# Four FF2 sections a layer and one more block pair in a two-layer decoder trunk

## The chip, the cores and the metric

The kernel runs on one core of a Trainium2 chip. The metric is device time in microseconds of one execution. TensorE (PE) multiplies, VectorE (DVE) and ScalarE (ACT) split, evacuate and activate, GpSimd (POOL) issues accumulating DMAs and takes a few small powers, and SyncE (SP) issues the plain DMAs.

## The reference

Sequence 512, model width 1024, FF width 2816, float32 throughout. Layer 0 mixes with dilated attention, layer 1 with causal pooling; each is followed by a SwiGLU block, which is where the change lies:

```python
def swiglu_ffn(h, w_gate_up, w_down):
    gu = h @ w_gate_up
    gate, up = gu[..., :D_FF], gu[..., D_FF:]
    return (jax.nn.silu(gate) * up) @ w_down

def reference(x, ...):
    for i in range(DEPTH):
        ...  # x = x + mixer(rmsnorm(x, g))
        x = x + swiglu_ffn(rmsnorm(x, ffn_norm[i]), w_ffn_gate_up[i], w_ffn_down[i])
    return rmsnorm(x, final_norm)
```

## The kernel before

**Arithmetic.** A float32 product is made of three products of rounded parts: every weight and every operand is split into a high part and a low rest (`split`: ACT writes the high part, DVE the rest), and `hi*hi`, `hi*lo`, `lo*hi` are added in PSUM. A *plain* product takes matmuls of 128x128 weights against 512 columns (`Product.add`). A *block* product (`chained`, with `mult`) works on 2x2 blocks and needs seven products of half size, with 256 columns each, instead of eight; in return ACT and DVE form sums of blocks of the weights and of the results.

**The FFN.** The width 2816 is 22 chunks of 128. `gate_up(j)` makes chunk j of the hidden activation: for j < `NPLAIN` as a plain pair (`plain_pair`: two plain products, 48 matmuls of 512 columns), else as a block pair (`strassen_pair`, 84 matmuls of 256 columns). FF2, the product with `w_down`, runs in sections given by `PARTS[layer]`, each `(first, end, block)`: gate/up runs up to the section's end (one chunk further before a block section), and then `down` adds the section's part of FF2 to the residual X. A plain section makes eight products (one per 128 output rows); a block section makes four `chained` calls, for two output chunks each. Block gate/up needs the normed input as blocks, which `prepare(k)` makes in four steps on DVE and ACT; a block FF2 section needs the hidden chunks as blocks (`operands`, `operands_right`, `operands_left`), which are put off (`late`) and run inside the next `chained`.

**Weights.** All weight tiles come through four rings: `raw` (4 buffers of 128x1024, where DMAs land), `rawhalf` (2), `w` (5 buffers for the split weights) and `half` (2). A plain unit is one load and one split. A block pair (`Pair`) is three SP loads `b`, `a`, `c`, a fourth, accumulating DMA issued by POOL that adds to `b` after it has landed, and four splits: `blocks` (of a), `sums` (of the accumulated b), `more` (a plus b, two DVE adds ahead of the split) and `last` (of c):

```python
nc.sync.dma_start(self.b, self.src[:, :2 * n])
nc.sync.dma_start(self.a, self.src[:, n:3 * n])
nc.sync.dma_start(self.c, self.src[:, :n])
nc.gpsimd.dma_start(self.b.rearrange("p (a c) -> p a c", a=2),
                    self.src[:, None, 3 * n:].to_broadcast([P, 2, n]), accum_op=OP.add)
```

`chained` uses them in the order b, s, m, b, s, m, l (first half of `blocks`, first half of `sums`, first half of `more`, then the second halves, then `last`).

**Order.** The source lists all units in the order of their use (`ffn_plan`). `pump`, called after each product, issues the loads whose buffers are free in the program's order and up to two splits; a scheduler then orders the instructions of each engine at build time, and each engine runs its own list in that order. A load waits on the chip until the last reader of its buffer (a DVE instruction) is done, and a split until the last matmul that reads its `w` buffer is.

**The end.** FF2's last section in layer 1 ends with two output chunks in halves of 256 columns (`ends`, `end`, `add`), so that the final norm and the output of the left half run beside the right half's products; `emit` scales and stores the left half, `turn_last` and the code after it transpose and store the right half.

Of the kernel before, what the change touches and what calls it, by code (L numbers as in the profile page):

```python
# [15 lines left out]
P = 128  # L16
S = 512
D = 1024
# [45 lines left out]
def trunk(ctx: ExitStack, tc: tile.TileContext, xT, norms, w_first, w_qk, w_qkp, w_v0, w_v0p, w_v12, w_out, w_pair, w_down, w_dblock, w_pin, w_pgrp,  # L64
# [171 lines left out]
    def ffn_plan(layer):  # L236
        j = 0
        for i, (first, end, block) in enumerate(PARTS[layer]):
            while j < min(end + block, FC):
                if j < NPLAIN:  # L240
                    plain_gu(layer, j)
                else:
                    pairs(w_pair[layer, j], shift=0, back=True)
                j += 1
            if block:
                for m in range(K2):
                    pairs(w_dblock[sum(p[2] for l in range(layer) for p in PARTS[l]) + sum(p[2] for p in PARTS[layer][:i]), m],
                          shift=0, back=True)
# [733 lines left out]
    with tc.tile_pool(name="fpool", bufs=2) as fpool:  # L982
# [24 lines left out]
        def ffn(layer, nxt, lead, row):  # L1007
# [6 lines left out]
            def plain_pair(j, up):  # L1014
                pg = gu()
                gt = ftile("gt")
                nc.vector.tensor_mul(gt, pg, row)
                pu = gu()
                if j == NPLAIN - 1:
                    for k in range(KC):  # L1020
                        give((op, k))
                nc.vector.tensor_mul(up, pu, row)
                nc.scalar.activation(gt, gt, AF.Silu)
                nc.vector.tensor_mul(up, up, gt)
# [89 lines left out]
            def gate_up(j, ahead):  # L1114
                first, block = next((p[0], p[2]) for p in PARTS[layer] if p[0] <= j < p[1])
                u = tmp.tile([P, S], F32, tag="sq", name="u", bufs=3) if block or ahead else ftile("up")
                i, odd = (j - first) // 2, j % 2
                if j < NPLAIN:
                    plain_pair(j, u)
                elif block and odd and j == FC - 1:  # L1120
                    strassen_pair(u, later(operands, i, U["even"]), later(operands_right, i, u))
                else:
                    strassen_pair(u)
                if j == FC - 1:
                    for key in [key for key in held if key[0] == "t"]:
                        give(key)
                if ahead and not block:
                    U["later"] = j, u
                elif not block:
                    keep(j, u)  # L1130
                elif not odd:
                    U["even"] = u
                elif j == FC - 1:
                    operands_left(i, u)
                else:
                    late.extend([later(operands, i, U["even"]), later(operands_right, i, u), later(operands_left, i, u)])
                if j < K2:
                    prepare(j)

# [9 lines left out]
            for first, end, block in PARTS[layer]:  # L1149
                while j < min(end + block, FC):  # L1150
                    gate_up(j, j == end)
                    j += 1
# [4 lines left out]
                if block:  # L1157
# [108 lines left out]

        ends = [[weights() for n in units_of(HALF)] for i in range(2)]
        halves = [slice(i * S // 2, (i + 1) * S // 2) for i in range(2)]

        def end(i, half, js, f=None):  # L1270
            f = f or Product(HALF, hidden, keep=ends[i])
            return f.add(js, cols=halves[half])

        def add(i, half, f):
            m, cols = KC - 2 + i, halves[half]
            nc.vector.tensor_add(X[m][:, cols], X[m][:, cols], f.p[:, cols])
# [34 lines left out]

        def total(half, sq):
            t = ftile("total", H2)
            nc.vector.tensor_add(t, acc[4][:, halves[half]], sq)
            return t
# [12 lines left out]
        turn_last(range(5))  # L1328
        sq = add(1, 1, f)
        scale_last(KC - 1, on_dve=True)  # L1330
# [93 lines left out]
```

## Time and profile before

| | |
|---|---|
| median of 3 runs | 1206.85 us (1206.4 to 1207.08) |
| profiled execution, its own time | 1206.44 us |
| its span | 1204.6 us |
| PE busy | 1193.7 us, 9720 matmuls |
| DVE busy | 966.3 us |
| ACT busy | 658.0 us |
| POOL busy | 138.7 us |
| HBM | 151 GB/s over the span |

Busy times are of the span of one profiled execution; the execution itself takes 1.8 us longer than the span. A row of a timeline gives the start in us from the start of the span, the duration, the engine, the line of the kernel, the operation, what it writes and reads, and in brackets how long the engine idled before it and what released it. SPq and POOLq are issues of DMAs. In a table of windows each engine has its busy time in the window with the number of instructions, then follow the TensorE clock that was granted (1.00 is full), the DMA share and the rate.

Where the parts of the program lie in the span: attention and its output projection up to 481 us, layer 0's FFN up to 806, the pooling mixer up to 874, layer 1's FFN and the final norm to the end.

### The profile page before, as it was taken

The page shows a single profiled execution, that of the slowest core. Times are in us where ns is not written, and L with a number is a line of the kernel's source. Part 1 is how long each engine was busy: PE and PEld are TensorE (multiplying, and loading weights), DVE is VectorE, ACT ScalarE, POOL GpSimd, SP SyncE. Part 2 cuts the span into 40 slices and gives each one's busy share as a digit, 9 for nine tenths or more (in the row PEclk, how much of TensorE's full clock was granted, in tenths as well). Part 3 has the DMA queues.
Part 4 walks back from the last instruction along what each step waited for, and adds up shares of the span by engine and source line. Part 5 has one row for each costly group of instructions (what it writes and reads, how often), then busy time and mean ns, then how long its engine had stood idle before and what let it go on. Part 6 is the DMA issues. An engine that isn't in the chain of part 4 may idle for free.

```text
span 1204.6 us, 24247 instructions
## 1 busy us (share of the span) xinstructions
PE 1193.7 (99%) x9720; PEld 1117.6 (93%) x9720; DVE 966.3 (80%) x1650; ACT 658.0 (55%) x1162; POOL 138.7 (12%) x131
## 2 busy tenths in 40 slices
PE   9999999999999999999999999999999999999997
PEld 7889999999999988888999999988788999999987
DVE  7888888878889854965898889989997898788633
ACT  6545554555556543542677567663443676566531
POOL 1111111111111100101111111000300111111000
PEclk9999999999999999999999999999999999999999
DMA  8346667666756532336677777644016677777322
GB/s 292 112 103 171 144 158 169 162 166 150 179 150 158 190 123 91 96 106 142 177 199 192 186 196 192 182 149 140 28 53 166 162 196 187 192 192 190 110 77 71
DMA packets 71152, 183.65 MB, mean 152 GB/s; under 512 B 7152, under 2 KB 8320, under 8 KB 71040
## 3 DMA queue, kind: packets, MB, share of 16 engines
q1 hardware_dynamic: 49824, 140.41, 35.7%
q0 software_dynamic: 21072, 41.43, 20.9%
q8 instruction: 76, 1.25, 0.4%
q14 instruction: 36, 0.29, 0.1%
q10 hardware_dynamic: 144, 0.26, 0.1%
HBM read 179.98 MB, written 2.10 MB: 151 GB/s over the span
## 4 chain that ended last, share of the span: by engine, by line
PE 91%; DVE 5%; issue 2%; ACT 1%; POOL 0%; DVEq 0%; POOLq 0%; DMA 0%; ACTq 0%
PE ps L424 17%; PE ps L425 17%; PE ps L426 17%; PE ps L294 9%; PE ps L295 9%; PE ps L297 9%; PE ps L595 2%; PE ps L597 2%; PE ps L596 2%; DVE w L93 1%; PE ps L807 1%; PE ps L679 1%; DVE s L1223 1%; PE ps L699 1%; PE ps L801 1%
## 5 line engine op out<-in xcount | busy, mean ns | idle before, releaser
L92 ACT ACTIVATE w<-raw 128x1024 fp32r<-128x1024 f32 (+3 forms) x303 | 309.8, 1028 | 258.3 <-PE ps L297 84.3
L93 DVE TENSOR_TENSOR w<-raw,w 128x1024 fp32r<-128x1024 f32 (+3 forms) x303 | 356.1, 1180 | 76.3 <-ACT w L92 72.3
L424 PE MATMUL ps<-far,w 128*128 128x256 f32 x860 | 236.7, 275 | 0.0
L425 PE MATMUL ps<-far,w 128*128 128x256 f32 x860 | 236.7, 275 | 0.0
L426 PE MATMUL ps<-far,w 128*128 128x256 f32 x860 | 236.6, 275 | 0.0
L425 PEld LDWEIGHTS ps<-far,w 128*128 128x128 f32 x860 | 161.5, 188 | 0.1
L424 PEld LDWEIGHTS ps<-far,w 128*128 128x128 f32 x860 | 161.5, 188 | 0.1
L426 PEld LDWEIGHTS ps<-far,w 128*128 128x128 f32 x860 | 161.4, 188 | 0.0
L424 PE MATMUL ps<-near,w 128*128 128x256 f32 x556 | 158.1, 284 | 1.5 <-ACT first L506 1.5
L425 PE MATMUL ps<-near,w 128*128 128x256 f32 x556 | 154.3, 278 | 0.0
L426 PE MATMUL ps<-near,w 128*128 128x256 f32 x556 | 154.3, 277 | 0.0
L295 PE MATMUL ps<-near,w 128*128 128x512 f32 (+1 forms) x364 | 137.7, 378 | 0.6 <-DVE near L357 0.6
L294 PE MATMUL ps<-near,w 128*128 128x512 f32 (+1 forms) x364 | 138.1, 380 | 0.0
L297 PE MATMUL ps<-near,w 128*128 128x512 f32 (+1 forms) x364 | 137.3, 378 | 0.0
L424 PEld LDWEIGHTS ps<-near,w 128*128 128x128 f32 x556 | 104.8, 188 | 2.5 <-ACT first L506 2.1
L425 PEld LDWEIGHTS ps<-near,w 128*128 128x128 f32 x556 | 104.6, 188 | 0.0
L426 PEld LDWEIGHTS ps<-near,w 128*128 128x128 f32 x556 | 104.5, 188 | 0.0
L160 POOL DMA_DIRECT2D raw<-w_pair x34 | 41.2, 1210 | 366.5 <-DMA raw<-w_pair 200.1
L295 PEld LDWEIGHTS ps<-near,w 128*128 128x128 f32 x364 | 68.5, 188 | 14.0 <-DVE near L357 1.7
L297 PEld LDWEIGHTS ps<-near,w 128*128 128x128 f32 x364 | 68.5, 188 | 12.8
L294 PEld LDWEIGHTS ps<-near,w 128*128 128x128 f32 x364 | 68.5, 188 | 12.5
L92 ACT ACTIVATE half<-rawhalf 128x512 fp32r<-128x512 f32 x75 | 47.2, 631 | 14.4 <-PE ps L426 12.3
(323 smaller groups left out, 2671.1 us busy)
## 6 DMA issues: line engine op xcount, KB each, us to landing
raw<-w_pair SPq DMA_DIRECT2D x78, 512.0 KB, 4.5
raw<-w_qkp SPq DMA_DIRECT2D x36, 512.0 KB, 4.2
raw<-w_pair POOLq DMA_DIRECT2D x34, 512.0 KB, 7.4
raw<-w_dblock SPq DMA_DIRECT2D x24, 512.0 KB, 4.1
raw<-w_v SPq DMA_DIRECT2D x18, 512.0 KB, 4.4
raw<-w_qkp POOLq DMA_DIRECT2D x18, 512.0 KB, 7.6
rawhalf<-w_pair SPq DMA_DIRECT2D x34, 256.0 KB, 5.1
raw<-w_dblock POOLq DMA_DIRECT2D x12, 512.0 KB, 7.5
```

Source lines behind the costliest of these rows:

```text
L92: nc.scalar.activation(hi, v, AF.Copy)
L93: nc.vector.tensor_tensor(lo, v, hi.bitcast(F32), op=OP.subtract)
L160: nc.gpsimd.dma_start(self.b.rearrange("p (a c) -> p a c", a=2), self.src[:, None, 3 * n:].to_broadcast([P, 2, n]), accum_op=OP.add)
L294: nc.tensor.matmul(self.p[:, cols], w[0][:, s], mh[:, cols], start=self.done == 0, stop=False)
L295: nc.tensor.matmul(self.p[:, cols], w[0][:, s], ml[:, cols], start=False, stop=False)
L297: nc.tensor.matmul(self.p[:, cols], w[1][:, s], mh[:, cols], start=False, stop=self.done == self.n)
L424: nc.tensor.matmul(dst, w.t[0][:, c], th, start=k == 0 and not on, stop=False, skip_group_check=on)
L425: nc.tensor.matmul(dst, w.t[0][:, c], tl, start=False, stop=False, skip_group_check=on)
L426: nc.tensor.matmul(dst, w.t[1][:, c], th, start=False, stop=k == n - 1, skip_group_check=on)
L595: nc.tensor.matmul(o, mh, wh, start=k == 0, stop=False)
L596: nc.tensor.matmul(o, mh, wl, start=False, stop=False)
L597: nc.tensor.matmul(o, ml, wh, start=False, stop=k == K2 - 1)
```

## The change

Layer 0's FF2 sections become 2 plain, 8 block, 6 block and 6 plain chunks (before: 6 plain, 8 block, 8 block); layer 1's become 2 plain, 8 block, 8 block and 4 plain (before: 4 plain, 8 block, 10 plain). The plain gate/up pairs of a layer go from five to four, so chunk 4 is now a block pair. All plain pairs now run before the first FF2 section (`max(end + block, NPLAIN)`), and `prepare(j)` stands inside plain pair j, between its gate and its up product, not behind the pair. At the end five output chunks, not two, are made in halves, and the squares of all five are summed half by half. On the host the block weights of a 6-chunk section are padded to the width of the others; the loads take only the used part.

```diff
-NPLAIN = 5
+NPLAIN = 4
...
-PARTS = {0: ((0, 6, False), (6, 14, True), (14, 22, True)), 1: ((0, 4, False), (4, 12, True), (12, 22, False))}
+PARTS = {0: ((0, 2, False), (2, 10, True), (10, 16, True), (16, 22, False)),
+         1: ((0, 2, False), (2, 10, True), (10, 18, True), (18, 22, False))}
+ENDS = 5
...
-            while j < min(end + block, FC):
+            while j < min(max(end + block, NPLAIN), FC):
...
                 for m in range(K2):
-                    pairs(w_dblock[...section..., m],
-                          shift=0, back=True)
+                    pairs(w_dblock[...section..., m, :,
+                                   :2 * (end - first) * P], shift=0, back=True)
...
             def plain_pair(j, up):
                 pg = gu()
                 gt = ftile("gt")
                 nc.vector.tensor_mul(gt, pg, row)
+                prepare(j)
                 pu = gu()
...
-                if j < K2:
-                    prepare(j)
...
-                while j < min(end + block, FC):
-                    gate_up(j, j == end)
+                while j < min(max(end + block, NPLAIN), FC):
+                    gate_up(j, block and j == end)
                     j += 1
...
-                for m in range(KC - 2 if nxt == 4 and last else KC):
+                for m in range(KC - ENDS if nxt == 4 and last else KC):
...
-        t = total(0, add(0, 0, end(0, 0, range(HALF))))
-        sq = add(1, 0, end(1, 0, range(HALF)))
-        f = end(0, 1, range(5))
+        t, late = (acc[4][:, cols] for cols in halves)
+        for i in range(ENDS):
+            sq = add(i, 0, end(i, 0, range(HALF)))
+            if i < ENDS - 1:
+                t = total(t, sq)
+        f = end(0, 1, range(HALF))
         r = rstd([t, sq])
-        end(0, 1, range(5, HALF), f)
-        t = total(1, add(0, 1, f))
-        f = end(1, 1, range(1))
+        t = total(late, add(0, 1, f))
+        t = total(t, add(1, 1, end(1, 1, range(HALF))))
+        f = end(2, 1, range(HALF // 2))
         emit(0, r)
-        for k in range(KC - 1):
+        for k in range(KC - ENDS + 2):
             scale_last(k)
-        f = end(1, 1, range(1, HALF), f)
+        t = total(t, add(2, 1, end(2, 1, range(HALF // 2, HALF), f)))
+        f = end(3, 1, range(HALF))
+        scale_last(KC - 3)
+        t = total(t, add(3, 1, f))
+        f = end(4, 1, range(HALF))
+        scale_last(KC - 2)
         turn_last(range(5))
-        sq = add(1, 1, f)
+        sq = add(4, 1, f)
         scale_last(KC - 1, on_dve=True)
```

More of the change, by code (lines that the diff above doesn't have):

```diff
@@ L246, in ffn_plan @@
                 for m in range(K2):
-                    pairs(w_dblock[sum(p[2] for l in range(layer) for p in PARTS[l]) + sum(p[2] for p in PARTS[layer][:i]), m],
-                          shift=0, back=True)
+                    pairs(w_dblock[sum(p[2] for l in range(layer) for p in PARTS[l]) + sum(p[2] for p in PARTS[layer][:i]), m, :,
+                                   :2 * (end - first) * P], shift=0, back=True)
             else:
@@ L1264, in trunk @@
         hidden, HALF = ffn(1, 4, lead, row)
-        ends = [[weights() for n in units_of(HALF)] for i in range(2)]
+        ends = {}
         halves = [slice(i * S // 2, (i + 1) * S // 2) for i in range(2)]
         def end(i, half, js, f=None):
+            if i not in ends:
+                ends[i] = [weights() for n in units_of(HALF)]
             f = f or Product(HALF, hidden, keep=ends[i])
@@ L1274, in add @@
         def add(i, half, f):
-            m, cols = KC - 2 + i, halves[half]
+            m, cols = KC - ENDS + i, halves[half]
             nc.vector.tensor_add(X[m][:, cols], X[m][:, cols], f.p[:, cols])
```

14 lines of the change are left out of this document (7 added, 7 removed).

## The prediction

> **What bounds the kernel now.** I read the page's totals and chain first, then stretches of the span with the granted clock, then single rows where a plain FF2 section hands over to block work.
>
> ```profile
> span 1204.6 us, 24247 instructions
> PE 1193.7 (99%) x9720; PEld 1117.6 (93%) x9720; DVE 966.3 (80%) x1650; ACT 658.0 (55%) x1162; POOL 138.7 (12%) x131
> PEclk9999999999999999999999999999999999999999
> ...
> PE 91%; DVE 5%; issue 2%; ACT 1%; POOL 0%; DVEq 0%; POOLq 0%; DMA 0%; ACTq 0%
> ```
>
> TensorE (PE) is busy for 99% of the span, at full clock in nearly every slice, and is 91% of the chain that ended last. So a change pays by what it takes off PE, and costs what it makes PE wait. What a matmul costs is read from stretches without waits.
>
> ```profile
> 486.28 0.39 PE L295 MATMUL ps<-near,w 128*128 128x512 f32 x1
> ...
> 499.21 0.39 PE L295 MATMUL ps<-near,w 128*128 128x512 f32 x1
> ...
> 600.00:785.00 185.00, 184.29 (x1617) 184.09 (x1616) 167.39 (x292) 126.25 (x226) 21.77 (x18) 1.00 0.73 191
> 944.00:1120.00 176.00, 176.00 (x1547) 176.00 (x1546) 150.94 (x250) 118.10 (x199) 21.73 (x18) 1.00 0.71 187
> ```
>
> Between the first two rows lie 57 starts of 512-wide matmuls: 12.93 / 57 = 0.2268 us each. The last row is a stretch of 256-wide matmuls alone (block work in layer 1): 176 / 1547 = 0.1138 us each. The third column is PE, the fifth DVE: 151 of 176 us, and 167 of 185 us in the stretch of layer 0. DVE is near PE there, but below it.
>
> **The change: work of PE.** Chunk 4 turns from a plain gate/up pair into a block pair, one a layer, and trades 48 wide matmuls for 84 narrow ones. Layer 0's FF2 goes from 16 block chunks to 14 (+48 wide, -84 narrow), layer 1's from 8 to 16 (-192 wide, +336 narrow). The halves at the end are 120 narrow matmuls before (2 chunks x 2 halves x 10 x 3) and after (5 x 2 x 4 x 3). In sum +420 narrow and -240 wide, which the order of the built program also gives: 420 x 0.1138 - 240 x 0.2268 = 47.8 - 54.4 = **-6.6 us**. All of it is on the path, since PE sets it.
>
> **A wait that goes.** Layer 0 ends before in a block section in which each step also carries the next norm's work on DVE; after, it ends in six plain chunks (4.1 us of PE per output chunk, 18 x 0.2268).
>
> ```profile
> L424 PE MATMUL ps<-near,w 128*128 128x256 f32 x556 | 158.1, 284 | 1.5 <-ACT first L506 1.5
> ```
>
> These 1.5 us of idle PE (three waits between 775 and 797 us) lie in that section: **-1.5 us**, from 0 if the next late thing takes their place.
>
> **A wait that comes: the first block pair after the short FF2 section.** After the change both layers run four plain pairs, then FF2 over two chunks, then the first block pair (chunk 4). Let T be the end of the last plain up product. FF2 over two chunks is 8 x 2 x 3 = 48 wide matmuls, 10.9 us; the pair's first product takes 12 x 0.1138 = 1.4 more. So PE wants the second product's weights, the "sums" of a pair, at T+12.3. Before, layer 0's first block pair came straight behind five plain pairs, its loads long issued, and layer 1's behind 21.8 us of FF2 (96 wide) and a plain pair.
>
> These sums need a chain that can't start early. The pair loads into the ring of four "raw" buffers behind the eight FF2 units; its first load (b) takes the buffer of unit five, whose split waits for the "w" buffer of the last gate/up weight, free at T. The nearest place in the trace is layer 1 after its first FF2 section, where the same steps run:
>
> ```profile
> 905.91 0.68 DVE L1022 TENSOR_TENSOR up<-ps,row 128x512 f32<-128x512 f32 x1
> 906.54 0.69 DVE L93 TENSOR_TENSOR w<-raw,w 128x512 fp32r<-128x512 f32 x1
> ...
> 912.39 0.69 DVE L93 TENSOR_TENSOR w<-raw,w 128x512 fp32r<-128x512 f32 x1
> 913.10 0.33 SPq L157 DMA_DIRECT2D raw<-w_pair  x1
> 915.33 0.33 SPq L158 DMA_DIRECT2D raw<-w_pair  x1
> 916.66 1.06 ACT L92 ACTIVATE w<-raw 128x1024 fp32r<-128x1024 f32 x1 [2.09 <-PE ps L297]
> 917.75 1.23 DVE L93 TENSOR_TENSOR w<-raw,w 128x1024 fp32r<-128x1024 f32 x1 [0.45 <-ACT w L92]
> 918.16 1.23 POOL L160 DMA_DIRECT2D raw<-w_pair  x1 [43.34 <-DMA raw<-w_pair]
> 919.01 0.33 SPq L157 DMA_DIRECT2D raw<-w_pair  x1
> 927.05 0.69 DVE L176 TENSOR_TENSOR raw<-raw 128x512 f32<-128x512 f32 x1 [2.67 <-DMA raw<-w_pair]
> ```
>
> The split ends at 913.08 and SP issues b at 913.10: the load does wait for the ring. POOL's accumulating DMA follows at 918.16 (5.1 us: it waits for b to land), and DVE has its result at 927.05 (8.9 us). Of all accumulating DMAs, and of the two in this window:
>
> ```profile
> DMA to landing us min/median/max: 6.4/7.5/10.3
> ...
> DMA to landing us min/median/max: 6.6/7.7/8.8
> ```
>
> Now the chain after the change. Unit five's split follows the up multiply (905.91 to 906.54, 0.6 us) and has 256 columns instead of 512 (0.35 us), so b goes out at T+1.0. Accumulate issued: T+6.1. Landed: T+14.9, with the 8.8 of the nearest place, where as here three more loads follow at once. ACT's half of the split 1.06: T+16.0. DVE's half 1.23: T+17.2. PE, which wanted it at T+12.3, stands 4.7 us in all.
>
> Then "more": two adds, with one X add between them, a split on ACT and one on DVE.
>
> ```profile
> L176 DVE TENSOR_TENSOR raw<-raw x1: 692/692/692, 927.0 to 927.0; 128x512 f32<-128x512 f32 x1
> L177 DVE TENSOR_TENSOR raw<-raw x1: 684/684/684, 928.3 to 928.3; 128x512 f32<-128x512 f32 x1
> ```
>
> 0.69 + 0.69 + 0.68 + 1.06 + 1.23 = 4.35 us, in which PE has only 24 narrow matmuls (2.7 us) and a few that stand interleaved (0.8): about 0.9 us more. Behind these splits in ACT's queue stand two more weight splits (2.1 us) and then the copy that frees the PSUM tile for the pair's fifth product, some 0.5 us late.
>
> One more wait follows from ACT's order in the built program. The split of the third pair's sums stands ahead of the second pair's first copy. The third pair's b takes the first pair's b buffer, free after its first add (T+17.9): issue T+18.0, accumulate T+23.1, landed T+30.6 (median 7.5; few other loads now), split T+31.7, copy T+32.0. PE, now 6 us late, wants it at T+29.5: 2.5 us. The fourth pair's chain is in time. Per layer 4.7 + 0.9 + 0.5 + 2.5 = 8.6 us, from 5.6 (landing 6.6 throughout) to 10.2 (8.8 throughout). Two layers: **+17 us**, 11 to 20.
>
> A rule of the Trainium skill speaks here: "DMA: Bandwidth & Descriptors", section "Anatomy of one DMA — SWDGE (gpsimd) path", puts a POOL-issued DMA at about 2.0 us plus its bytes over 436 GB/s, so 512 KB would be an estimated 3.2 us, which would take the stall away. The trace does not agree: no accumulating DMA landed in less than 6.4 us.
>
> **Clock.** Waits of several us are new to PE here.
>
> ```profile
> 1198.00:1200.00 2.00, 0.00 (x1) 0.00 (x0) 1.41 (x2) 1.27 (x2) 1.05 (x2) 0.94 0.21 71
> 1200.00:1204.60 4.60, 0.00 (x0) 0.00 (x0) 0.00 (x1) 0.00 (x0) 0.00 (x0) 0.50 0.61 228
> ```
>
> After PE's last matmul at 1198 the granted clock is 0.94 over two us and then 0.50: it can halve within two us of idling. How long it stays low once PE resumes no row shows. From nothing (the idle is short, and PE waits again anyway) to the 2.7 us of work between two waits run at half speed (2.7 us a layer): I take **+1 us** for both layers, 0 to 5.4. The skill's "TensorE: Matmul & The Clock Gate", section "Part 1: The HAM clock gate", has an idle window of about 3.4 us, free-running; by it the 3.7 us wait would halve the clock in many runs.
>
> **The rest.** Preparation moves inside the pairs: the same instructions, in the built order now all ahead of the last up multiply, where before three splits of 512 columns (0.6 us each, by the row at 906.54) came behind it. Against these 1.8 us DVE saves 0.25 us on each of four narrower FF2 splits and has a pair's 10.9 us of PE work as cover. Cost 0; if the cover failed, up to 1.8 us a layer. Layer 1's further block sections load DVE as in the 944 to 1120 stretch: 0. At the very end DVE's eight output scalings stand ahead of the last three adds, before it was one:
>
> ```profile
> 1193.02 2.83 DVE L1287 SCALAR_TENSOR_TENSOR x<-x,nrm,ps 128x256 f32<-128x256 f32 x7
> 1195.76 0.41 DVE L1276 TENSOR_TENSOR x<-x,ps 128x256 f32<-128x256 f32 x1
> ```
>
> The last add began where the scalings ended; two more adds and totals may lengthen the tail: **+0.5 us**, 0 to 1.5.
>
> **Sum.** The profiled execution took 1206.44 us (span 1204.6), 0.4 under the median of 1206.85. 1206.4 - 6.6 - 1.5 + 17 + 1 + 0.5 = 1216.8; beside the median **1217 us**.
>
> **Rivals.**
> 1. *Faster: the accumulate lands in time.* The first split must be ready at T+12.3, so the landing may take 12.3 - 1.06 - 6.1 = 5.1 us at most; then only -6.6 - 1.5 + 0.5 remain: 1199. Against it, the smallest of 75 is 6.4; for it, the DMA queues are emptier than on average. Chance 0.10.
> 2. *Half the wait.* PE's interleaved matmuls, or loads released earlier than I read, cut the stall to 4 us a layer: 1206.4 - 8.1 + 8.5 = 1207. Chance 0.08.
> 3. *More waits.* ACT's order makes a third pair wait, or DVE (167 of 185 us in layer 0's block stretch) becomes the bound over layer 1's new block section; 8.8 us throughout (+20), the clock's full 5.4 and the tail's 1.5 give 1225; a DVE that is 3% too slow over 150 us of block work adds 4.5 more. Chance 0.15.
>
> **How the numbers follow.** The forecast has 0.67, and its own range runs from 1210 (11 us of stall) to 1221. The range that leaves out under 2 in 10 reaches from rival 2 to rival 3: 1207 to 1226; below lie rival 1 and a little. A difference under 0.2% (2.4 us) can't be told from none. Faster: 0.12 (rival 1 and the low part of rival 2); same 0.04; slower 0.84.
>
> **What would show it.** In the changed profile: two PE waits of over 2 us a layer, at the second product of chunk 4's pair and the third of chunk 5's, put down to ACT's weight split and copy, with POOL's accumulate landing 6.5 to 9 us after issue; DVE and ACT idle there too; 420 more narrow and 240 fewer wide matmuls; no PE wait at layer 0's end. If PE runs through chunk 4 without a wait, the prediction is wrong.

## The result: 1225.6 us against 1206.6, and where the profile shows the loss

The changed kernel takes 1225.60 us (median of 4 runs, 1224.94 to 1228.61) against 1206.62 us before (4 runs, 1206.27 to 1207.08). The ratio is 1.0161, 95% interval 1.0148 to 1.0173. The forecast was 1217, with 1207 to 1226 as its range: the side was right and the stall was where it was placed, but 9 us were missing. The profiled execution took 1225.7 us. Its page has these totals and this chain:

```profile
span 1223.9 us, 24860 instructions
PE 1198.1 (98%) x9900; PEld 1128.4 (92%) x9900; DVE 1002.9 (82%) x1747; ACT 680.2 (56%) x1227; POOL 146.7 (12%) x137
PEclk9999999999999999989999999999999999999999
...
PE 82%; DMA 6%; DVE 6%; issue 3%; ACT 1%; POOL 1%; POOLq 0%; DVEq 0%; ACTq 0%; SPq 0%
```

PE has 180 matmuls more (420 narrow more, 240 wide fewer), and one slice of the span shows a clock below 0.9. DMA, 0% of the chain that ended last before, is 6% of it now: PE waits for loads. The stretches of the span show where. First after, then before (columns: stretch, PE, PE weight loads, DVE, ACT, POOL, granted clock, DMA share, GB/s):

```profile
500.00:600.00 100.00, 94.27 (x674) 88.32 (x674) 87.35 (x160) 57.75 (x107) 10.95 (x9) 0.97 0.64 161
...
700.00:770.00 70.00, 67.73 (x589) 66.94 (x589) 57.66 (x92) 43.39 (x76) 7.26 (x6) 1.00 0.74 187
770.00:900.00 130.00, 128.79 (x669) 105.44 (x668) 104.01 (x182) 59.95 (x89) 14.59 (x11) 1.00 0.31 97
900.00:1000.00 100.00, 91.99 (x646) 85.87 (x645) 85.34 (x154) 57.24 (x103) 10.89 (x9) 0.97 0.61 155
```

```profile
500.00:600.00 100.00, 100.00 (x624) 89.84 (x623) 73.86 (x117) 47.74 (x77) 7.24 (x6) 1.00 0.48 127
...
700.00:770.00 70.00, 70.00 (x620) 70.00 (x619) 66.01 (x122) 51.70 (x95) 9.01 (x8) 1.00 0.74 190
770.00:900.00 130.00, 127.29 (x737) 106.79 (x736) 116.66 (x207) 66.30 (x108) 15.25 (x12) 1.00 0.34 103
900.00:1000.00 100.00, 100.00 (x715) 93.24 (x714) 83.83 (x143) 57.85 (x99) 10.89 (x9) 1.00 0.66 168
```

Before, PE never stood in 500 to 600 and 900 to 1000 us; after, it stands 5.7 and 8.0 us there, and the granted clock averages 0.97 over these stretches. They hold the hand-overs, from a layer's plain pairs over the short FF2 section to its first block pairs. A third, smaller loss (2.3 us) has come at 700 to 770, in layer 0's section of 6 block chunks, and 1.5 us have gone at 770 to 900, layer 0's end.

A finer measure, used below: over all rows of PE I add up the time from one matmul's start to the next, less 0.2268 us (512 wide) or 0.1138 us (256 wide; the few narrower ones in proportion). That is the time PE lost, whether it stood or ran slowly. By it the profiled execution has 6.6 us less PE work, and loses 10.0 us more at layer 0's hand-over (500 to 600), 12.8 more at layer 1's (900 to 1000), 2.5 more at 700 to 780, 1.6 less at 780 to 900, 0.9 more at 1000 to 1180, 0.4 more at the end and 0.8 more before 500: 19.2 us in sum, and the two profiled executions differ by 19.3 (1225.7 - 1206.44).

The chain at chunk 4's pair in layer 0, from the timeline of after, engine by engine (start, duration, engine, line; in brackets the idle time before and what ended it):

```profile
517.40 0.33 SPq L159 DMA_DIRECT2D raw<-w_pair  x1
534.70 0.33 SPq L159 DMA_DIRECT2D raw<-w_pair  x1
522.03 1.27 POOL L162 DMA_DIRECT2D raw<-w_pair  x1 [37.12 <-DVE w L95]
538.92 1.21 POOL L162 DMA_DIRECT2D raw<-w_pair  x1 [10.07 <-DMA raw<-w_pair]
531.71 1.06 ACT L94 ACTIVATE w<-raw 128x1024 fp32r<-128x1024 f32 x1 [6.15 <-DMA raw<-w_pair]
546.53 1.06 ACT L94 ACTIVATE w<-raw 128x1024 fp32r<-128x1024 f32 x1 [0.37 <-DMA raw<-w_pair]
532.79 1.23 DVE L95 TENSOR_TENSOR w<-raw,w 128x1024 fp32r<-128x1024 f32 x1 [4.78 <-ACT w L94]
533.94 0.68 DVE L178 TENSOR_TENSOR raw<-raw 128x512 f32<-128x512 f32 x1
532.82 0.58 PE L426 MATMUL ps<-far,w 128*128 128x256 f32 x1 [4.23 <-ACT w L94]
```

The load of b, the first buffer of the pair, goes out at 517.40, 1.1 us behind the end of the plain pairs (516.3). POOL's accumulate follows 4.6 us later, ACT can split the sums (b once the accumulate has landed) 9.7 us after that, and PE stands 4.23 us for this split. The third pair's b goes out at 534.70, as soon as the first "more" add (533.94 + 0.68) has left its buffer. The other waits of PE over 1 us in the hand-overs and the 6-chunk section, then the accumulate and ACT's split that stand behind the last of them:

```profile
725.24 0.39 PE L426 MATMUL ps<-near,w 128*128 128x256 f32 x1 [1.57 <-ACT first L500]
932.92 0.38 PE L426 MATMUL ps<-far,w 128*128 128x256 f32 x1 [3.30 <-ACT w L94]
949.02 0.38 PE L426 MATMUL ps<-far,w 128*128 128x256 f32 x1 [1.59 <-ACT first L500]
960.98 0.38 PE L426 MATMUL ps<-far,w 128*128 128x256 f32 x1 [2.12 <-ACT first L500]
```

```profile
949.44 1.20 POOL L162 DMA_DIRECT2D raw<-w_pair  x1 [8.51 <-ACT first L500]
958.57 1.06 ACT L94 ACTIVATE w<-raw 128x1024 fp32r<-128x1024 f32 x1 [3.71 <-DMA raw<-w_pair]
```

Three of them are for ACT's first copy (line 500). It stands in ACT's queue behind the split of the next pair's sums, and that split waits for a DMA: 3.71 us at 958.57, which is 9.1 us behind the accumulate of that pair.

### The profile page after: what moved, and what is told of

Read it like the earlier page. It is cut to its first block, busy times and chain, and to the rows that moved or that the text cites. A ratio compares the mean times of both kernels' runs of the same rounds, so it can differ in the third digit from the quotient of the medians.

```text
span 1223.9 us, 24860 instructions
## 1 busy us (share of the span) xinstructions
PE 1198.1 (98%) x9900; PEld 1128.4 (92%) x9900; DVE 1002.9 (82%) x1747; ACT 680.2 (56%) x1227; POOL 146.7 (12%) x137
## 4 chain that ended last, share of the span: by engine, by line
PE 82%; DMA 6%; DVE 6%; issue 3%; ACT 1%; POOL 1%; POOLq 0%; DVEq 0%; ACTq 0%; SPq 0%
PE ps L426 17%; PE ps L428 17%; PE ps L427 17%; PE ps L296 7%; PE ps L299 7%; PE ps L297 7%; DMA raw<-w_pair 6%; PE ps L597 2%; PE ps L599 2%; PE ps L598 2%; DVE w L95 2%; PE ps L809 1%; PE ps L681 1%; DVE s L1224 1%; ACT w L94 1%
## 5 line engine op out<-in xcount | busy, mean ns | idle before, releaser
L94 ACT ACTIVATE w<-raw 128x1024 fp32r<-128x1024 f32 (+3 forms) x317 | 316.5, 1005 | 253.4 <-PE ps L428 71.1
L95 DVE TENSOR_TENSOR w<-raw,w 128x1024 fp32r<-128x1024 f32 (+3 forms) x317 | 363.5, 1152 | 85.3 <-ACT w L94 81.5
L426 PE MATMUL ps<-far,w 128*128 128x256 f32 x896 | 250.7, 280 | 13.0 <-ACT w L94 7.8
L428 PE MATMUL ps<-far,w 128*128 128x256 f32 x896 | 249.1, 278 | 1.2 <-DVE w L95 1.2
L427 PE MATMUL ps<-far,w 128*128 128x256 f32 x896 | 249.2, 278 | 0.0
L426 PEld LDWEIGHTS ps<-far,w 128*128 128x128 f32 x896 | 170.9, 191 | 15.5 <-ACT w L94 8.4
L426 PE MATMUL ps<-near,w 128*128 128x256 f32 x628 | 178.0, 283 | 1.6 <-ACT first L500 1.6
L427 PE MATMUL ps<-near,w 128*128 128x256 f32 x628 | 174.3, 278 | 0.0
L428 PE MATMUL ps<-near,w 128*128 128x256 f32 x628 | 174.2, 277 | 0.0
L428 PEld LDWEIGHTS ps<-far,w 128*128 128x128 f32 x896 | 170.3, 190 | 1.7 <-DVE w L95 1.7
L427 PEld LDWEIGHTS ps<-far,w 128*128 128x128 f32 x896 | 170.9, 191 | 0.1
L297 PE MATMUL ps<-near,w 128*128 128x512 f32 (+1 forms) x332 | 125.3, 377 | 0.6 <-DVE near L359 0.6
L296 PE MATMUL ps<-near,w 128*128 128x512 f32 (+1 forms) x332 | 125.7, 379 | 0.0
L299 PE MATMUL ps<-near,w 128*128 128x512 f32 (+1 forms) x332 | 124.9, 377 | 0.0
L426 PEld LDWEIGHTS ps<-near,w 128*128 128x128 f32 x628 | 118.3, 188 | 2.1 <-ACT first L500 1.8
L427 PEld LDWEIGHTS ps<-near,w 128*128 128x128 f32 x628 | 118.2, 188 | 0.0
L428 PEld LDWEIGHTS ps<-near,w 128*128 128x128 f32 x628 | 118.1, 188 | 0.0
L297 PEld LDWEIGHTS ps<-near,w 128*128 128x128 f32 x332 | 62.5, 188 | 12.9 <-DVE near L359 1.8
L299 PEld LDWEIGHTS ps<-near,w 128*128 128x128 f32 x332 | 62.5, 188 | 11.3
L296 PEld LDWEIGHTS ps<-near,w 128*128 128x128 f32 x332 | 62.5, 188 | 11.3
L94 ACT ACTIVATE half<-rawhalf 128x512 fp32r<-128x512 f32 (+1 forms) x81 | 50.4, 623 | 12.5 <-PE ps L428 10.6
```

What stands on the lines that cost most here:

```text
L94: nc.scalar.activation(hi, v, AF.Copy)
L95: nc.vector.tensor_tensor(lo, v, hi.bitcast(F32), op=OP.subtract)
L296: nc.tensor.matmul(self.p[:, cols], w[0][:, s], mh[:, cols], start=self.done == 0, stop=False)
L297: nc.tensor.matmul(self.p[:, cols], w[0][:, s], ml[:, cols], start=False, stop=False)
L299: nc.tensor.matmul(self.p[:, cols], w[1][:, s], mh[:, cols], start=False, stop=self.done == self.n)
L426: nc.tensor.matmul(dst, w.t[0][:, c], th, start=k == 0 and not on, stop=False, skip_group_check=on)
```

## The experiments

Each kernel starts from the changed one unless said otherwise. The lost PE time is by the measure above, from each run's profiled execution (its time is the column "profiled us"). In e2 the added matmuls count as work, not as lost time. A few tenths either way are the rounding of the two costs.

| run | median us | profiled us | 500-600 | 700-780 | 780-900 | 900-1000 | from 1000 |
|---|---|---|---|---|---|---|---|
| before | 1206.6 | 1206.4 | -0.1 | 0.7 | 7.5 | -0.1 | 3.5 |
| after | 1225.6 | 1225.7 | 9.9 | 3.2 | 5.9 | 12.7 | 4.8 |
| e1 no sum in 3 pairs | 1214.4 | 1214.3 | 4.2 | 7.0 | 5.8 | 4.5 | 4.7 |
| e2 PE filled | 1228.8 | 1226.5 | 6.0 | 2.4 | 5.8 | 5.5 | 5.1 |
| e3 pair ahead | 1224.0 | 1224.2 | 9.3 | 6.3 | 5.8 | 8.9 | 4.7 |
| e4 four first | 1211.1 | 1214.5 | 3.0 | 6.3 | 5.8 | 2.3 | 8.3 |
| e5 fourth product first | 1247.5 | 1247.8 | 12.3 | 7.4 | 6.2 | 15.7 | 13.6 |
| e6 e4 with e5 | 1228.5 | 1230.3 | 4.9 | 4.5 | 6.4 | 4.4 | 16.6 |
| e7 no section of 6 | 1221.2 | 1221.5 | 11.5 | 0.7 | 5.8 | 9.9 | 4.7 |
| e8 layer 0 back | 1211.8 | 1211.6 | 0.3 | 0.7 | 7.4 | 10.0 | 4.6 |
| e9 no sum in pair 4 | 1219.6 | 1217.3 | 6.1 | 3.7 | 5.8 | 8.9 | 4.7 |
| e10 block first | 1207.1 | 1206.6 | 0.3 | 0.7 | 7.4 | 6.8 | 3.5 |
| e11 rest of the change | 1205.8 | 1205.6 | 0.3 | 0.7 | 7.4 | 0.9 | 3.9 |
| e12 block first, late | 1202.2 | 1202.0 | 0.2 | 0.7 | 7.4 | 3.2 | 3.5 |

### e1: is it the accumulating load?

```
+            if self.plain_sums:      # the pairs of chunks 4, 5 and 6
+                return
             nc.gpsimd.dma_start(self.b.rearrange(...), ..., accum_op=OP.add)
```

> The changed kernel without the accumulating DMA of the block pairs of chunks 4, 5 and 6 in both layers: the sums of these six pairs hold two corners of the weights instead of the sums with the other two (this part of the computation is left out). All other instructions stay. Theory (ring chain: the sums can't be split before POOL's accumulate has landed, about 14 us after the end of the plain pairs): the sums of chunk 4's pair are then ready when b has landed, about 5 us after the load goes out, before PE wants them; all waits of the hand-over (10.1 us in layer 0 and 12.9 in layer 1, slow clock included) go: 1225.6 - 23 = 1202 to 1205 us. Rival (the order of ACT's queue or DVE's load makes the waits): at most the first wait gets shorter, 1215 to 1222.

Measured 1214.44 us, ratio to before 1.0064 (1.0049 to 1.0079): between the theory and the rival, next to the rival's 1215. Of the 22.6 us that the two hand-overs lose, 13.9 went. What is left is mostly the wait for the "more" weights (0.8 and 1.6 us) and one behind the sums of a later pair, which still accumulates (1.3 and 1.6). But the 6-chunk section took 3.8 us back. In the built program the order of each of PE, ACT and DVE is that of the changed kernel, so the gain at the hand-overs is that of the missing accumulates, through the chain or through the traffic that they take from the other loads, which this run can't part. They are the larger part of the hand-over's loss, not all of it, and a gain in one place was partly paid back in the other.

### e2: does the slow clock cost?

```
         def behind(i):
             ...
+            for r in range(fill.get(i, 0)):
+                nc.tensor.matmul(beta, wb.t[0][:, :P], T["11", 0][0], start=True, stop=True)
```

> The changed kernel with PE kept busy where it waits: matmuls of 128 x 256 whose result is overwritten, 37 behind the first product of chunk 4's pair and 6 behind its second in layer 0 (4.2 and 0.7 us), 30 and 8 there in layer 1, and 14 and 18 in layer 1's next two pairs (1.6 and 2.0 us). Nothing waits for less. Theory (about 6 us of the loss is the granted clock, which falls in the wait and stays low for 4 to 8 us behind it): the granted clock stays at 1.00 from 528 to 540 us and from 929 to 966 us, and the time falls by 5 to 6 us: 1219 to 1221. Rival (the work behind the wait is slow for another reason, late operands among them, or was not slow at all): 1225 to 1228, as the fill only takes the place of the wait.

Measured 1228.76 us (1226.30 to 1231.15), ratio 1.0181 (1.016 to 1.0202): the rival's side. The clock around layer 0's wait, in stretches of after and then of the filled kernel, with two matmuls of the latter:

```profile
532.00:536.00 4.00, 2.72 (x11) 2.43 (x12) 3.21 (x5) 1.42 (x4) 0.00 (x0) 0.50 0.44 84
536.00:540.00 4.00, 4.00 (x25) 4.00 (x25) 2.74 (x6) 3.44 (x5) 1.08 (x1) 0.65 0.48 162
```

```profile
532.00:536.00 4.00, 3.27 (x27) 2.88 (x25) 3.75 (x7) 1.41 (x4) 0.00 (x0) 1.00 0.56 108
536.00:540.00 4.00, 2.76 (x13) 2.56 (x14) 3.82 (x5) 2.89 (x5) 1.20 (x1) 0.75 0.54 157
```

```profile
536.48 0.39 PE L427 MATMUL ps<-far,w 128*128 128x256 f32 x1 [0.81 <-ACT w L95]
...
537.74 0.40 PE L429 MATMUL ps<-far,w 128*128 128x256 f32 x1 [0.76 <-DVE w L96]
```

In the filled kernel PE runs at full clock up to 536, reaches the "more" product early and waits for its weights until 537.74. But the fill changed more than the clock. In the built program of the changed kernel, 8 matmuls of the pair's fourth product (6 in layer 1) stand ahead of the third, which uses the "more" weights, and the other 4 (6) behind its first two matmuls. With the fill, the third product follows the second and the fill directly, and the fourth comes behind. The rows show it: in after, DVE's add behind the fourth product comes ahead of ACT's copy behind the third; in the filled kernel (the last two rows below) it comes after it.

```profile
539.31 0.42 DVE L512 TENSOR_TENSOR gt<-ps,first 128x256 f32<-128x256 f32 x1 [1.08 <-PE ps L428]
540.79 0.37 ACT L508 COPY first<-ps 128x256 f32<-128x256 f32 x1 [1.34 <-PE ps L428]
```

```profile
540.09 0.38 ACT L511 COPY first<-ps 128x256 f32<-128x256 f32 x1 [1.21 <-PE ps L429]
542.18 0.42 DVE L515 TENSOR_TENSOR gt<-ps,first 128x256 f32<-128x256 f32 x1 [0.68 <-PE ps L429]
```

So PE came to the "more" weights with less work in between, and lost 1.9 us at them in layer 0 and 2.4 in layer 1. The gain of 5 to 6 us that the theory named did not appear: the lost time fell by 11.1 us at the two hand-overs, and the fill took 12.9. But the run does not show that the slow clock costs nothing, since a gain of some 4 us and these waits would cancel each other.

The rows of after allow an argument, which no run tested. The slow matmuls of layer 0 (534.5 to 538.7 us) and the first slow ones of layer 1 (935.0 to 938.1) lie ahead of a first copy (547.50 and 948.61). That copy stands in ACT's queue behind the split of the third pair's sums, and this pair's b went out at 534.70 and 935.40, released by an add of DVE and not by PE. With faster matmuls PE would have waited there for longer. Behind the third slow stretch (962.2 to 965.4, 1.6 us lost) PE loses nothing more up to 1000 us, so there the slow clock may have cost the whole 1.6 us.

### e3: is the load only issued too late?

```
                     pairs(w_pair[layer, j], shift=0, back=True)
+                    if j == NPLAIN:
+                        loads.insert(len(loads) - 1 - 1, loads.pop())
```

> The changed kernel with one thing moved: the loads of chunk 4's pair (b, a, c and the accumulate) stand one unit earlier, ahead of the eighth FF2 unit's load instead of behind it. So b takes the raw buffer of FF2 unit four, whose split waits for a weight that PE leaves one product (5.4 us) before the last plain up product. Theory (ring chain): b goes out about 4.4 us before that end instead of 1.0 behind it, the accumulate lands about 5.4 us earlier, the sums are ready at about the time when PE wants them: first wait 4.4 and 3.5 us down to 0 to 1, and most of the 6 us of clock with it: 1225.6 - 8 - 1 - 5 = 1211 us, 1207 to 1214; the third and fourth pairs' waits in layer 1 (1.8 and 2.3) may stay. Rival (the DMA queues are what is late, an earlier issue only lands later): 1222 to 1226.

Measured 1224.0 us, ratio 1.014 (1.0125 to 1.0155), inside the rival's range. The rival's reason, an earlier load that only lands later, holds for the third pair alone. Rows of its timeline:

```profile
511.93 0.33 SPq L159 DMA_DIRECT2D raw<-w_pair  x1
530.10 0.33 SPq L159 DMA_DIRECT2D raw<-w_pair  x1
544.66 1.06 ACT L94 ACTIVATE w<-raw 128x1024 fp32r<-128x1024 f32 x1 [3.11 <-DMA raw<-w_pair]
547.06 0.52 PE L428 MATMUL ps<-far,w 128*128 128x256 f32 x1 [3.63 <-ACT first L502]
```

b goes out 5.5 us earlier, as meant, and the first wait falls from 4.2 us to below 1 (one of 1.6 us for the first copy follows it). But the third pair's load goes out only 4.6 us earlier (530.10), and it takes 14.6 us until ACT can split its sums (544.66; 11.8 in after), so that 1.9 us of the lead are left. PE, now earlier, waits 3.63 us there for the copy behind that split. In layer 1 the two waits for first copies are 2.3 and 2.4 us, and the 6-chunk section loses 3.1 us more. The wait moved on. The edit also changed the built order: in this kernel two more operations of ACT (1.0 us) stand between that split and that copy than in after, so not all of the 3.63 us is the load's.

### e4: the same sections, with four plain chunks first

```
-PARTS = {0: ((0, 2, F), (2, 10, T), (10, 16, T), (16, 22, F)), 1: ((0, 2, F), (2, 10, T), (10, 18, T), (18, 22, F))}
+PARTS = {0: ((0, 4, F), (4, 12, T), (12, 18, T), (18, 22, F)), 1: ((0, 4, F), (4, 12, T), (12, 20, T), (20, 22, F))}
```

> The changed kernel with the FF2 sections in another place and the same amount of PE work: layer 0 has 4 plain, 8 block, 6 block, 4 plain chunks, layer 1 has 4 plain, 8 block, 8 block, 2 plain (2, 8, 6, 6 and 2, 8, 8, 4 in the changed kernel). The four plain pairs are then followed by 21.8 us of FF2 instead of 10.9. Theory (what is lost is lost where 10.9 us of cover are too short for a chain of 17 us): the hand-over's 23 us go, the waits of the section of 6 block chunks (3.5 us) stay: 1202 to 1206. Rival (more block sections cost by DVE's load or the clock, wherever they stand): 1215 or more.

Measured 1211.07 us, ratio 1.0034 (1.0021 to 1.0046). With 21.8 us of cover the first wait is gone and the hand-overs lose 3.0 and 2.3 us instead of 9.9 and 12.7; 17 of 23 us came back. The 6-chunk section lost 3 us more than in after, and the end 3.5 more, where PE waits 1.3 us for DVE's last totals behind halves of two chunks and 1.9 us for ACT's last scalings. The theory named the right place and left out the other two. (The profiled execution is the slowest of six, 3.4 us over their median.)

### e5 and e6: can PE give the sums more time?

```
         mult(alpha, wb, 0, T, "11", n)
+        mult(beta, wb, 1, T, "21", n)
         mult(gamma, ws, 0, T, "1", n)
         mult(alpha, wm, 0, T, "2", n, on=True)
-        mult(beta, wb, 1, T, "21", n)
         mult(alpha, ws, 1, T, "3", n, on=True)
```

> The changed kernel with one product moved in every block pair of the FFN: the fourth of the seven (the second half of the first weights, which needs neither the sums nor the 'more' weights) is done as the second, so PE wants the sums and the freed PSUM tile of the first copy 1.4 us later each (12 matmuls x 0.1138), the 'more' weights the same as before after the sums. No instruction is added or left out. Theory (the waits are deadlines missed by the load chain and by ACT's fixed order, each of some 0.4 to 4.4 us): every 'sums' wait falls by 1.4 us (4.4 to 3.0, 3.5 to 2.1), and the waits for the first copy (1.8, 2.3, 1.7 and four of 0.4 to 0.6) fall by 1.4 or go: 1225.6 - 2.8 - 5.5 = 1217 us, 1214 to 1220. Rival (PE's waits only move, since what ends last is the throughput of the load chain, about 7 to 8 us for each pair against 9.6 of PE work): 1222 to 1226.

> The FF2 sections of the run with four plain chunks first (4, 8, 6, 4 and 4, 8, 8, 2; 1211.1 us) with the fourth product done as the second as in the run beside it. Theory (deadlines): of its waits for the first copy (0.9, 0.4, 1.4, 4.0, 0.9, 0.6) 1.4 us each goes, about 5.5 us: 1205 to 1206 us. Rival (throughput of the load chain): 1209 to 1212.

Measured 1247.52 us, ratio 1.0341 (1.0323 to 1.0358), and 1228.53, ratio 1.0184 (1.0169 to 1.02). Both expectations failed, by 30 and 23 us. The first waits did fall as forecast (2.9 and 2.1 us). But in the old order no two products in a row go into the same PSUM tile; in the new one two products of alpha do, with ACT's copy of it between them, and PE waits for a copy in nearly every pair. The stretch of 600 to 700 us holds block work only; after has 100.00 us of PE in it, e5:

```profile
600.00:700.00 100.00, 98.69 (x838) 96.72 (x837) 84.64 (x145) 59.85 (x112) 12.07 (x10) 1.00 0.72 177
```

These are 38 matmuls fewer in the same 100 us (after: 876), 4.3 us, about 0.4 a pair. The edit carried a cost of its own in every pair, so it tells nothing of the rival; only the first wait's 1.4 us a product is confirmed.

### e7: the section of 6 block chunks

```
-PARTS = {0: (..., (10, 16, True), (16, 22, False)), ...
+PARTS = {0: (..., (10, 18, True), (18, 22, False)), ...
```

> The changed kernel with 8 instead of 6 block chunks in layer 0's third section and 4 instead of 6 plain ones in the last (2, 8, 8, 4 in both layers). PE work: 84 narrow matmuls more and 48 wide fewer, 9.6 - 10.9 = -1.3 us. Theory (in a section of 6 block chunks a block step takes 63 narrow matmuls, 7.2 us, too short for the load chain of 13 to 15 us for two pairs in flight; with 8 chunks it is 9.6 us): the waits of 720 to 750 us (3.4 us in all) go as well: 1225.6 - 1.3 - 3 = 1221 us. Rival (the waits there belong to the hand-over from block steps to gate/up pairs, whatever their length): 1224 to 1225.

Measured 1221.16 us, ratio 1.0115 (1.01 to 1.0131), as the theory had it. That it meets the theory to 0.2 us is partly luck: the hand-overs moved too, by +1.6 us in layer 0 and -2.8 in layer 1. The stretch of 700 to 770 us has its full PE time again:

```profile
700.00:770.00 70.00, 70.00 (x611) 70.00 (x610) 58.83 (x95) 44.06 (x75) 8.46 (x7) 1.00 0.71 185
```

In after, the pair behind the section has these rows:

```profile
710.37 0.33 SPq L159 DMA_DIRECT2D raw<-w_pair  x1
715.85 1.20 POOL L162 DMA_DIRECT2D raw<-w_pair  x1 [8.35 <-DVE w L95]
723.08 1.06 ACT L94 ACTIVATE w<-raw 128x1024 fp32r<-128x1024 f32 x1 [2.12 <-DMA raw<-w_pair]
```

From the load of b to the split are 12.7 us, where a block step of 6 chunks gives 63 x 0.1138 = 7.2 us of PE. In the kernels with this section the stretch of 700 to 780 us lost from 2.4 to 7.4 us, and 0.7 in those without it; what sets it in this range was not tried.

### e8: layer 0's sections as before

```
-PARTS = {0: ((0, 2, False), (2, 10, True), (10, 16, True), (16, 22, False)),
+PARTS = {0: ((0, 6, False), (6, 14, True), (14, 22, True)),
```

> The changed kernel with layer 0's FF2 sections as they were before (6 plain, 8 block, 8 block), still with four plain gate/up pairs; layer 1 as changed. Chunk 4's block pair then follows the plain pairs with no FF2 between, with its loads ahead of those of FF2. Theory (the stall belongs to the short FF2 section, whose eight loads stand ahead of the pair's): layer 0's hand-over (10.0 us) and the 6-chunk waits (2.5 us more than before) go, the waits of layer 0's end come back (+1.7), 1.3 us of PE work less: 1225.6 - 10 - 2.5 + 1.7 - 1.3 = 1213.5 us; a wait at chunk 4 straight behind the plain pairs would be 0 to 3. Rival (four plain pairs give too little lead for the first block pair wherever FF2 stands): 1218 to 1224.

Measured 1211.79 us, ratio 1.005 (1.0034 to 1.0067), 1.7 from the theory. With four plain pairs and no FF2 units ahead of chunk 4's loads, layer 0's hand-over loses 0.3 us; layer 1's still loses 10.0 (12.7 in after). The two layers' losses are largely separate.

### e9: one accumulate left out

```
-        units[-1][0].plain_sums = j in (4, 5, 6)
+        units[-1][0].plain_sums = j == 4
```

> The changed kernel without the accumulating DMA of chunk 4's pair alone, in both layers (its sums hold two corners of the weights only; this part of the computation is left out); the pairs of chunks 5 and 6 accumulate as before (left out too in the run that took 1214.4 us). Theory A (one late start is handed on: pair 6's load takes the buffer that pair 4's 'more' add frees, so an earlier pair 4 brings all the later loads forward): nearly the same gain as with three left out, the waits for the first copy of pairs 5 and 6 fall too: 1214 to 1217 us. Theory B (each pair's chain is too slow for PE by itself, so PE only meets the next pair's wait): the first wait goes and the waits at pairs 5 and 6 grow to 2 to 4 us: 1219 to 1223 us.

Measured 1219.60 us (1217.29 to 1222.72), ratio 1.0108 (1.0088 to 1.0127): theory B's range, with the profiled execution at 1217.3 between the two. The first wait went (4.2 to 0.7 us). Waits of later pairs in it:

```profile
543.02 0.38 PE L429 MATMUL ps<-far,w 128*128 128x256 f32 x1 [1.52 <-ACT first L503]
...
941.19 0.38 PE L429 MATMUL ps<-far,w 128*128 128x256 f32 x1 [2.00 <-ACT first L503]
952.84 0.38 PE L429 MATMUL ps<-far,w 128*128 128x256 f32 x1 [1.81 <-ACT first L503]
```

In layer 0 the wait at the second pair grew (0.3 to 1.5 us), in layer 1 the two stayed (1.6 and 2.1 in after). The built order of PE, ACT and DVE is that of the changed kernel here too. An earlier first pair does not clear those behind it. My reading is that with two pairs in flight in four raw buffers each next pair's sums are near their limit by themselves.

### e10, e11, e12: the change without a short FF2 section

e10 lets the four plain pairs feed the first block section; e12 is e10 without the two lines marked:

```
-PARTS = {0: ((0, 2, False), (2, 10, True), (10, 16, True), (16, 22, False)),
-         1: ((0, 2, False), (2, 10, True), (10, 18, True), (18, 22, False))}
+PARTS = {0: ((0, 6, False), (6, 14, True), (14, 22, True)),
+         1: ((0, 8, True), (8, 16, True), (16, 22, False))}
 ...
-                t = tmp.tile([P, S], F32, tag="row", name="t", bufs=1)
+                t = ftile("t") if i < U.get("plain", 0) else tmp.tile([P, S], F32, tag="row", name="t", bufs=1)
 ...
+                U["plain"] = (NPLAIN - first) // 2
 ...
+                    while j < NPLAIN and late:         # e10 only
+                        late.popleft()()               # e10 only
```

> A version without a short FF2 section: layer 0 as it was before (6 plain, 8 block, 8 block, as in the run of 1211.8 us), layer 1 with 8 block, 8 block, 6 plain chunks, where the outputs of the four plain gate/up pairs become operands of the first block section. Chunk 4's pair then follows the plain pairs with no FF2 units between in both layers, and 16 block chunks a layer remain: PE work as in that run (some 8 us under the kernel before). Theory (the stall belongs to the short FF2 section): layer 1's hand-over of about 10 us goes too: 1201 to 1204 us, faster than the kernel before by 3 to 5. Rival (four plain pairs and the operands on DVE and ACT beside them bring waits of their own, or the late chain meets chunk 4 anyway): 1207 to 1214.

e11 is the changed kernel with `PARTS = {0: ((0, 6, F), (6, 14, T), (14, 22, T)), 1: ((0, 6, F), (6, 14, T), (14, 22, F))}`.

> The rest of the change without its new section lengths: four plain gate/up pairs with the preparation inside them and five chunks in halves at the end, but FF2 in sections of 6 plain, 8 block, 8 block chunks in layer 0 (as before) and 6 plain, 8 block, 8 plain in layer 1 (before: 4, 8, 10; as many block chunks). PE work against the kernel before: 168 narrow matmuls more and 96 wide fewer for the two chunks that turn into block pairs, 19.1 - 21.8 = -2.7 us; the halves give and take nothing. Theory (everything lost by the change is lost at the short FF2 section and the one of 6 block chunks): no new wait of PE over 0.5 us, 1206.8 - 2.7 = 1204 us, 1203.5 to 1205.5. Rival (four plain pairs, the preparation on DVE or the longer halves cost by themselves): 1207 to 1210.

> The version of 1207.1 us (layer 0: 6 plain, 8 block, 8 block; layer 1: 8 block, 8 block, 6 plain) with the operands of the first four chunks of layer 1 made behind the products of the first block pairs instead of inside the plain pairs, where DVE was busy for 100% of 880 to 920 us. Theory (layer 1's 7 us of waits there come from DVE, which is late with the weight splits): most of the 7 us goes, as the same DVE work lies where DVE has 1 to 2 us of room a pair: 1202 to 1204.5 us, faster than both kernels. Rival (the load chain is what is late, or DVE's work only moves): 1206 to 1208.

Measured: e10 1207.07 us, ratio 1.0007 (0.9997 to 1.0017), the rival's end; e11 1205.79, ratio 0.999 (0.9981 to 0.9999); e12 1202.23, ratio 0.9962 (0.9949 to 0.9974), faster than both kernels. Their stretches of layer 1's first block pairs, in this order:

```profile
900.00:1000.00 100.00, 96.81 (x798) 94.43 (x797) 90.70 (x157) 64.27 (x115) 12.07 (x10) 1.00 0.70 175
```

```profile
900.00:1000.00 100.00, 99.74 (x709) 92.82 (x708) 76.04 (x121) 52.03 (x86) 8.46 (x7) 1.00 0.57 150
```

```profile
900.00:1000.00 100.00, 98.98 (x834) 97.39 (x833) 92.37 (x165) 63.50 (x119) 10.86 (x9) 1.00 0.73 178
```

e11 lies 0.3 us above the theory's range and below the rival's. It shows that the rest of the change, four plain pairs with the preparation inside and longer halves, is no loss: it is 1.2 us faster than before, 1.5 less than the PE work alone would give (about 2 us of small waits came with it). e12 keeps all the PE work that the change saves and has PE standing 1.0 us here instead of 8.0. Between e10 and e12 only the place of the operands differs, and 3.6 us of lost PE time between 900 and 1000 us went with it. DVE is full in both; from 880 to 920 us, e10 and then e12:

```profile
880.00:920.00 40.00, 39.46 (x228) 34.55 (x227) 39.99 (x77) 22.20 (x43) 1.23 (x2) 1.00 0.32 67
```

```profile
880.00:920.00 40.00, 40.00 (x243) 35.65 (x242) 39.85 (x71) 24.37 (x44) 2.41 (x2) 1.00 0.48 106
```

So the gain is not that DVE got air, as expected: it is as full as before, and only its order has changed. In e10 PE loses 0.7 and 0.6 us to weight splits at 920 to 922 us and 1.8 to a first copy at 933; in e12 it loses at most 0.5 us at a time before 940 us. That the weights come ahead of the operands in e12 is my reading of this and was not tried by itself.

## Why the prediction was right about the place and wrong about the size

- **PE work, -6.6.** Right: -6.6 by the rows, with the matmul counts as forecast.
- **The wait that goes, -1.5.** It went (-1.6 at 780 to 900). The step allowed that another late thing takes its place but priced that at up to 0: the 6-chunk section, which the sum did not price, lost 2.5 us more. e7 shows the section's length as its cause.
- **First wait at chunk 4's pair, 4.7 a layer.** Right: 4.4 and 3.5 us, by the chain as laid out: b 1.1 us behind the end of the plain pairs, the accumulate 4.6 later, the split 9.7 (layer 0) and 9.0 (layer 1) later, where I had used 8.8. The Trainium skill's "DMA: Bandwidth & Descriptors", section "Anatomy of one DMA — SWDGE (gpsimd) path", would still give an estimated 3.2 us for it; the profile's landing times of line 162 in after disagree again:

```profile
DMA to landing us min/median/max: 6.1/7.5/9.7
```

- **"More" and the copy behind it, 1.4, and clock, +1 for both layers.** 1.9 a layer together; the rows lose 3.3 and 3.1 between the first wait and 540 (layer 0) or 940 us (layer 1), slow matmuls and waits taken together. The clock did fall to 0.50 (in layer 1 twice, where matmuls start 0.21 us apart from 934.96 to 937.09 and from 962.20 to 965.18). How much of this is the clock's own cost stays open: e2 changed the order of the products along with the clock, and by the rows of after much of the slow work lay ahead of a wait that the loads set.
- **The second pair's copy, 2.5 a layer.** 0.4 and 1.8 us lost: the order of ACT's queue works as described, with a smaller price.
- **"The fourth pair's chain is in time."** Wrong in layer 1, and the step that failed most: ACT waited 3.71 us for its sums (958.57), PE 2.12 for the copy behind, and 1.6 us went to slow matmuls after it. From 940 us on layer 1 loses 6.1 us where the sum had 2.5. In layer 0 the same copy cost PE a wait of 0.3 us. In layer 1 that pair's accumulate went out 7.1 us after its b, and its split began 9.1 us after that; in layer 0 these were 5.5 and 7.5, and the sum has 5.1 and 7.5 for a late pair. Why both took longer in layer 1 was not tried. I had followed the chain up to the third pair and taken the next to have caught up; e3 and e9 show waits at later pairs too, though the first was earlier.
- **Hand-overs together, 17 + 1.** Measured 10.0 and 12.8 more than before, 4.8 us over the forecast. With the 6-chunk section (2.5), the rest of layer 1's block work (0.9, priced at 0) and 0.8 before the change's place, that is 9 us, the error.
- **Tail, +0.5; preparation, 0.** +0.4; and PE has 10.00 of 10 us in the plain pairs of both layers (492 to 502 and 890 to 900) although DVE is full there. e11 has no new wait there either.
- **Rival 3** (a third pair waits too) was nearest, 1225 us at a chance of 0.15. Its part that held is ACT's order and the late chain, with the third pair's wait over 2 us in layer 1 only. Its clock part, the full 5.4 us, is near what the slow matmuls come to by the rows (about 5 us), but no run shows how much of that reached the time. That the number came near is in part luck, since DVE did not become the bound and the 6-chunk section is not in it.

Of what should show it: two waits over 2 us in each layer came only in layer 1 (3.30, 2.12), and the second of these at the pair behind the one named; layer 0 had one (4.23); ACT and DVE idle there (6.15 and 4.78 us) and the counts came; the 9.7 us from the accumulate to the split in layer 0 were over the 6.5 to 9.

## What to carry to other kernels

A wait at the end of a chain of loads is not one number: when the buffers hold two steps and each step's chain is about as long as two steps' compute, a late start can be met again at the next steps, so price the chain for every step until it has caught up, and price each section by whether its step is longer than the chain's rate. Before cutting a section shorter, ask which loads stand behind it in a ring; feeding the plain outputs into a block section (e12) kept the saved matmuls without a short section. Before putting a price on a stalled engine's slow clock, look for what the engine has to wait for next: where that is late too, faster work would only end in a longer wait, an argument that no run here tested. An added instruction can change the built order along with what it was meant to change, as in e2.

## What the hardware showed that I had not expected

The granted clock fell without a long wait. In e2 PE had at most 0.81 us of idle time at a stretch (536.48 and 537.74), yet matmuls started 0.21 us apart from 538.15 to 541.13 us instead of 0.1138, and came back at 541.4. The Trainium skill's "TensorE: Matmul & The Clock Gate", section "Part 1: The HAM clock gate", puts both the idle window and the busy time to return at about 3.4 us; in e2 the return agrees (3.4 us from 537.97), while the fall came after about 2 us (535.7 to 537.7) with two matmuls in them, shorter than that window. In after's layer 0 the return took longer: PE resumed at 532.82 and its matmuls were slow until 538.72, 5.9 us, with one wait of 0.46 us in them.
